# Entry of the up-projection: the copy of the third pair's product 5 ahead of the fifth pair's plain rounding on ACT

## The chip, the cores and the metric

The kernel runs on one core of one Trainium2 chip. The metric is the device time of one execution in microseconds; the median of three runs of the kernel before is 912.32 us.

## What the kernel computes

One layer of a streaming encoder on 512 tokens of width 1024: a recurrent branch and an attention branch, merged and projected, then a feed-forward block. The part that matters here is the beginning of the feed-forward block:

```
h = rms_norm(x, ffn_norm_pre[layer])
up = jnp.einsum("bsd,df->bsf", h, w_up[layer])          # 1024 -> 6144 columns
up = causal_dwconv(up, conv_f_w[layer], conv_f_b[layer]) # 3 taps over the tokens
gate, val = jnp.split(up, 2, axis=-1)
ffn_out = jnp.einsum("bsf,fd->bsd", jax.nn.gelu(gate) * val, w_down[layer])
x = x + rms_norm(ffn_out, ffn_norm_post[layer])
```

Of the kernel before, what the change touches and what calls it, by code (L numbers as in the profile page):

```python
# [63 lines left out]
def kernel(  # L64
# [263 lines left out]
    X, Y = slice(0, SH), slice(SH, S)  # L328
# [593 lines left out]
    with ExitStack() as g2:  # L922
# [17 lines left out]
        p, n = gp[0], gp[1]  # L940
# [239 lines left out]
    with ExitStack() as mix:  # L1180
# [116 lines left out]
        with ExitStack() as later:  # L1297
            for i in turned[NT - 1]:
                later.enter_context(tc.issue_after(i.ins))
            p = pairs[NU]  # L1300
# [61 lines left out]
    def first_tap(j):  # L1362
        fe[j] = [tap(e, first[2 * j + i][0], t) for i, (e, t) in enumerate(((j, "cg"), (j + JF, "cv")))]

    def first_taps(j, *which):
        for i in which or (0, 1):
            taps(j + JF * i, first[2 * j + i][0], fe[j][i])
# [7 lines left out]
    p, n = pairs[NU], pairs[NU + 1]  # L1375
# [18 lines left out]
    p.add(p.a[:, X], p.a[:, X], 2)  # L1394
    first_tap(0)
    n.sums_lo(1)
    m.plain_low(0)
    m.plain_high(0)
    p.p5()
    p.keep(1, p.c[:, X])  # L1400
    first_taps(2)
    first_taps(0, 0)
    m.sums(0)
# [64 lines left out]
    with man2:  # L1468
# [3 lines left out]
        b, p = pairs.pop(JF - 2), pairs.pop(JF - 1)  # L1472
# [274 lines left out]
```

## The kernel before

Every float32 operand of a product is split into a high half (rounded) and a low half (the rest), and each product is three matmuls: high by high, high by low, low by high. The result lies with channels on the 128 partitions and tokens along the free axis.

The 48 column blocks of the up-projection, each 128 wide, are worked on as 24 pairs: block j of the gate with block j + 24 of the value. Pairs 0 to 2 are computed plainly (their banks are `up0`, `up24`, `up1`, `up25`, `up2`, `up26`). From pair 3 on, a pair is computed by a two-by-two scheme with seven products in place of eight, over the halves of the contraction and of the tokens (X is the first 256 tokens, Y the last 256). Each of the seven products is 12 matmuls of 128x128 by 128x256: eight that use a high weight half (lines 429 and 430, alternating) and four that use a low one (line 432). Pairs 3, 4 and 5 are called p, n and m at the entry of this stage. In the names below the last number is the pair: `ml0_5` is a tile of pair 5; `th0_4` of pair 4. A number behind that, where there is one, only counts tiles.

Each pair has two PSUM banks, `a` (`up3` for pair 3) and `c` (`up27` for pair 3). What the code calls:

- `plain(i)`, that is `plain_low(i)` and `plain_high(i)`: the rounding of the untransformed weights. `plain_low(0)` makes ACT write the negated weights into `ml0` (line 364) and then makes GpSimd issue a DMA that adds the weights to it (line 365); `plain_high(0)` makes ACT write the rounded weights into `mh0` (line 380). Products 1 and 2 of a pair read `mh0` and `ml0`; product 3 reads `mh1` and `ml1`.
- `sums`, `sums_hi`, `sums_lo`: sums of weight blocks on DVE (`t`, line 325), their high halves on ACT (`th`, line 411) and low halves on DVE (`tl`, line 325). Products 4 to 7 read these.
- `p12`, `p5`, `product(n, ...)`: the matmuls. `p12` puts product 1 in `a[Y]` and product 2 in `a[X]`; `p5` puts product 5 in `c[X]`.
- `keep(i, ps)`: ACT copies a half bank into a tile `x` in SBUF (line 436), as that half bank is going to be accumulated further. `keep(2)` saves product 1, `keep(1)` saves product 5, `keep(0)` saves the sum after product 6.
- `add`: DVE adds a kept tile to a half bank (line 448).
- `tap`, `taps`: ACT starts the three-tap convolution out of PSUM (line 1325), DVE adds the other two taps (line 1331). `first_tap`, `first_taps` and `first_glu` do this for pairs 0 to 2.

From here on the order is written out by hand: instructions go to their engines in the order in which the code issues them. At the entry it is (lines 1396 to 1402, after `p.p12()`, `p.keep(2, ...)`, the add, `first_tap(0)` and `n.sums_lo(1)`):

```
    m.plain_low(0)
    m.plain_high(0)
    p.p5()
    p.keep(1, p.c[:, X])
    first_taps(2)
    first_taps(0, 0)
    m.sums(0)
```

Then a loop runs `period` (line 454) once for each pair. For pair 3 it issues product 6 into `a[Y]`, `keep(0)`, `n1.plain(1)` (nothing is left to do of it here, pair 4's is done), product 3 into `c[X]`, pair 4's `p12` and `keep(2)`, and product 7. For each later pair it issues `p5`, the adds of the pair before, the tap of the bank before, `keep(1)`, product 6, `keep(0)`, product 4 of the pair before, product 3, the next pair's `p12` and product 7. Product 3 accumulates onto product 5 in `c[X]`, so it has to wait until `keep(1)` has read that half bank.

## Time and profile before

| | |
|---|---|
| median of 3 runs | 912.32 us (912.11 to 912.33) |
| the profiled execution's own time | 910.93 us |
| its span (first to last instruction) | 909.2 us |
| PE (matmul) busy | 899.7 us, 99% of the span |
| DVE busy | 736.5 us, 81% |
| ACT busy | 596.3 us, 66% |
| POOL (GpSimd) busy | 214.8 us, 24% |
| granted TensorE clock | 0.999 of full speed |

The span leaves out 1.73 us of the profiled execution's time, and the profiled execution is 1.39 us shorter than the median of the runs. Times in the rows of the profile are microseconds from the span's start. PE is TensorE's matmul side, PEld its weight loads. In a row of the timeline stand the start, the duration, the engine, the line, the operation, what is written and read, how many instructions were merged, and in brackets the idle time of the engine before it with what ended it. The ends of matmuls are modelled.

### The profile page before, as it was taken

Reading aid. Unit: us, or ns where it says so; the run is one execution under the profiler, and the core shown is the slowest. Engines: PE = TensorE matmul, PEld = TensorE weight load, DVE = VectorE, ACT = ScalarE, POOL = GpSimd, SP = SyncE. Lnnn points to the kernel's source line nnn. Section 1 sums busy time; section 2 is a strip of 40 time slices with the busy share of each in tenths; the row PEclk is TensorE's granted clock in tenths of the full one; section 3 lists DMA queues with packets and bytes.
Section 4 is the critical chain, followed back from the end, with each engine's and each line's share of the span. In section 5 each row is a group of like instructions: output and inputs, shape, how many; then the busy total and the mean of one; then the engine's idle time right before and its main releaser. Section 6 shows DMA issues by size and latency. Waiting matters only on the chain.

```text
span 909.2 us, 15828 instructions
## 1 busy us (share of the span) xinstructions
PE 899.7 (99%) x5858; PEld 801.4 (88%) x5858; DVE 736.5 (81%) x1204; ACT 596.3 (66%) x1032; POOL 214.8 (24%) x276
## 2 busy tenths in 40 slices
PE   9999999999999999999999999999999999999997
PEld 8888888878899998888888889999999999988886
DVE  6975469538878749888868588989999999889897
ACT  7564595333466648776654487878888888677564
POOL 3244335544110112212104100233323223100000
PEclk9999999999999999999999999999999999999999
DMA  6777589989865378444515664678888988699764
GB/s 261 263 237 195 159 221 272 247 215 197 196 161 161 101 245 280 143 143 149 177 45 183 200 185 139 140 185 209 235 210 215 244 203 210 209 400 324 244 203 145
DMA packets 71040, 185.24 MB, mean 204 GB/s; under 512 B 7153, under 2 KB 27681, under 8 KB 70578
## 3 DMA queue, kind: packets, MB, share of 16 engines
q1 hardware_dynamic: 47360, 127.72, 42.0%
q0 software_dynamic: 23456, 56.37, 28.7%
q8 instruction: 46, 0.75, 0.3%
q14 instruction: 32, 0.26, 0.1%
q10 hardware_dynamic: 146, 0.14, 0.0%
HBM read 150.69 MB, written 35.73 MB: 205 GB/s over the span
## 4 chain that ended last, share of the span: by engine, by line
PE 98%; ACT 1%; DMA 1%; DVE 0%; issue 0%; SPq 0%; DVEq 0%
PE up L429 7%; PE up L430 7%; PE up L432 7%; PE dn L1455 4%; PE dn L1456 4%; PE dn L1454 4%; PE ga L220 2%; PE ga L219 2%; PE pa L220 2%; PE pa L218 2%; PE pa L219 2%; PE ga L218 2%; PE k L218 2%; PE q L218 2%; PE wo L1170 2%; PE pb L218 2%
## 5 line engine op out<-in xcount | busy, mean ns | idle before, releaser
L1331 DVE SCALAR_TENSOR_TENSOR u<-up,cpt,u 128x511 f32<-128x511 f32 x96 | 71.3, 745 | 3.5 <-ACT u L1325 1.8
L365 POOL DMA_DIRECT2D ml<-raw_up x42 | 36.2, 863 | 153.6 <-ACT ml L364 87.2
L1456 PE MATMUL dn<-wh_dn,al 128*128 128x512 f32 (+1 forms) x180 | 67.6, 376 | 0.0
L1455 PE MATMUL dn<-wl_dn,ah 128*128 128x512 f32 (+1 forms) x180 | 67.5, 375 | 0.0
L1454 PE MATMUL dn<-wh_dn,ah 128*128 128x512 f32 (+1 forms) x180 | 67.5, 375 | 0.0
L429 PE MATMUL up<-sh,th 128*128 128x256 f32 x252 | 60.2, 276 | 0.0
L430 PE MATMUL up<-sl,th 128*128 128x256 f32 x252 | 60.2, 276 | 0.0
L175 DVE TENSOR_TENSOR wl_dn<-raw_dn,wh_dn 128x1024 fp32r<-128x1024 f32 x42 | 51.1, 1217 | 8.2 <-ACT wh_dn L172 8.2
L172 ACT CAST wh_dn<-raw_dn 128x1024 fp32r<-128x1024 f32 x42 | 44.1, 1051 | 20.2 <-issue 8.0
L1325 ACT ACTIVATE u<-up,cpt 128x512 f32<-128x512 f32 x48 | 37.0, 779 | 21.7 <-PE up L432 11.9
L325 DVE TENSOR_TENSOR tl<-t,th 128x1024 fp32r<-128x1024 f32 x42 | 51.1, 1217 | 0.0
L429 PEld LDWEIGHTS up<-sh,th 128*128 128x128 f32 x252 | 47.3, 188 | 0.0
L430 PEld LDWEIGHTS up<-sl,th 128*128 128x128 f32 x252 | 47.3, 188 | 0.0
L1339 POOL TENSOR_TENSOR yf<-u,u 128x512 f32<-128x512 f32 x23 | 30.7, 1334 | 62.8 <-issue 48.2
L411 ACT CAST th<-t 128x1024 fp32r<-128x1024 f32 x42 | 43.7, 1044 | 2.5 <-DVE t L325 0.4
L429 PE MATMUL up<-h2h,mh 128*128 128x256 f32 x168 | 40.2, 276 | 0.0
L430 PE MATMUL up<-h2l,mh 128*128 128x256 f32 x168 | 40.2, 276 | 0.0
L1456 PEld LDWEIGHTS dn<-wh_dn,al 128*128 128x128 f32 x180 | 33.9, 188 | 6.3 <-DVE al L325 0.3
L1454 PEld LDWEIGHTS dn<-wh_dn,ah 128*128 128x128 f32 x180 | 33.9, 188 | 6.1
L1455 PEld LDWEIGHTS dn<-wl_dn,ah 128*128 128x128 f32 x180 | 33.9, 188 | 6.0
L432 PE MATMUL up<-sh,tl 128*128 128x256 f32 x252 | 38.8, 276 | 0.0
L1015 ACT ACTIVATE P<-P,mx 128x384 f32<-128x384 f32 (+3 forms) x64 | 35.2, 553 | 5.1 <-DVE mx L1010 4.2
(724 smaller groups left out, 3218.9 us busy)
## 6 DMA issues: line engine op xcount, KB each, us to landing
raw_up<-in_w_up_dram SPq DMA_DIRECT2D x48, 512.0 KB, 5.4
td<-in_w_down_dram POOLq DMA_DIRECT2D x36, 512.0 KB, 6.3
raw_dn<-td SPq DMA_DIRECT2D x24, 512.0 KB, 5.3
ml<-raw_up POOLq DMA_DIRECT2D x21, 512.0 KB, 5.5
B<-cnd POOLq DMA_DIRECT2D x16, 640.0 KB, 5.4
raw_dn<-in_w_down_dram SPq DMA_DIRECT2D x18, 512.0 KB, 4.2
raw_wo<-in_w_out_dram SPq DMA_DIRECT2D x16, 512.0 KB, 4.3
td<-td POOLq DMA_DIRECT2D x12, 512.0 KB, 11.2
```

What stands on the lines that cost most here:

```text
L172: act.copy(self.wh, self.raw)
L175: engine.tensor_tensor(out=self.wl, in0=self.raw, in1=self.wh.bitcast(F32), op=ALU.subtract)
L218: pe.matmul(dst, ah, bh, start=first, stop=False)
L325: dve.tensor_tensor(out=out, in0=a, in1=b, op=ALU.subtract)
L411: act.copy(self.th[i], self.t[i])
L429: pe.matmul(dst, wh[:, k], ah[:, k], start=first and k == 0, stop=False, skip_group_check=True)
L430: pe.matmul(dst, wh[:, k], al[:, k], start=False, stop=False, skip_group_check=True)
L432: pe.matmul(dst, wl[:, k], ah[:, k], start=False, stop=k == KH - 1, skip_group_check=True)
L1331: dve.scalar_tensor_tensor(out=c[:, s:], in0=ps[:, : S - s], scalar=col(C_CFW + 3 * e + j), in1=c[:, s:], op0=ALU.mult, op1=ALU.add)
L1454: pe.matmul(d[:, x], ah[:, k, tok], wh[:, k, x], start=first, stop=False, skip_group_check=True)
L1455: pe.matmul(d[:, x], ah[:, k, tok], wl[:, k, x], start=False, stop=False, skip_group_check=True)
L1456: pe.matmul(d[:, x], al[:, k, tok], wh[:, k, x], start=False, stop=last, skip_group_check=True)
```

## The change

Two lines are moved. The matmuls of pair 3's product 5 and the copy `keep(1)` are issued ahead of pair 5's plain rounding, where they stood behind it.

```
     first_tap(0)
     n.sums_lo(1)
+    p.p5()
+    p.keep(1, p.c[:, X])
     m.plain_low(0)
     m.plain_high(0)
-    p.p5()
-    p.keep(1, p.c[:, X])
     first_taps(2)
     first_taps(0, 0)
```

On ACT, at the entry of the up-projection (`u0` and `u24` are pair 0's taps, `up27` is bank `c` of pair 3, `x1_3` the copy of its product 5, `x0_3` the copy of bank `a` after product 6, `x2_4` the copy of pair 4's product 1):

```order
 L1325 ACTIVATE u0_6819<-up0_6243,cpt_79 128x512
 L1325 ACTIVATE u24_6821<-up24_6268,cpt_79 128x512
-L364 ACTIVATE ml0_5_6825<-raw_up5_6777 128x1024
-L380 CAST mh0_5_6828<-raw_up5_6777 128x1024
-L436 COPY x1_3_6843<-up27_6830 128x256
+L436 COPY x1_3_6838<-up27_6825 128x256
+L364 ACTIVATE ml0_5_6840<-raw_up5_6777 128x1024
+L380 CAST mh0_5_6843<-raw_up5_6777 128x1024
 L436 COPY x0_3_6866<-up3_6791 128x256
 L436 COPY x2_4_6905<-up4_6880 128x256
```

The copy of product 5 moved ahead of two instructions, and these two moved behind one; all else on ACT stands as before.

On POOL, at the same place (`ml0_5` is the DMA that completes the low half whose rounding moved on ACT; `yf` are the products of gate and value of pairs 1, 2 and 0):

```order
 L365 DMA ml1_4_6772<-raw_up28_6527 128x512
 L1339 TENSOR_TENSOR yf1_6788<-u1_6756,u25_6758 128x512
-L365 DMA ml0_5_6825<-raw_up5_6777 128x1024
+L365 DMA ml0_5_6840<-raw_up5_6777 128x1024
 L1339 TENSOR_TENSOR yf2_6911<-u2_6764,u26_6766 128x512
 L1339 TENSOR_TENSOR yf0_6915<-u0_6819,u24_6821 128x512
```

Nothing moved there but the numbers that count tiles, since the DMA stands between the same two instructions. PE, DVE and SP (the queue of plain loads) also keep their order.

More of the change, by code (lines that the diff above doesn't have):

```diff
@@ L1396 @@
     n.sums_lo(1)
+    p.p5()
+    p.keep(1, p.c[:, X])
     m.plain_low(0)
     m.plain_high(0)
-    p.p5()
-    p.keep(1, p.c[:, X])
     first_taps(2)
```

## Prediction

> **What bounds the kernel now.** I read the chain that ended last first, then the waits of PE from the up-projection on, then the busy time of each engine by stretches.
>
> The chain, by engine:
>
> ```profile
> PE 98%; ACT 1%; DMA 1%; DVE 0%; issue 0%; SPq 0%; DVEq 0%
> ```
>
> The kernel ends when TensorE has gone through its matmuls, so a microsecond counts only if PE stands still for it. ACT's 1% is small, and the question is whether this change touches a piece of it. The list of PE's waits from 540 us to the end (engine, line, what it waited for, total, times, longest) has one row:
>
> ```profile
> PE up L429 <- ACT x L436: 1.2, 1, 1.2
> ```
>
> It is a matmul of line 429 that waited for a copy of line 436, once. The busy times of the stretches show what surrounds it (start and end, length, then busy time per engine with the number of instructions):
>
> ```profile
> 565.00:592.00 27.00, 25.76 (x228) 25.56 (x226) 24.83 (x37) 23.68 (x35) 5.66 (x6) 1.00 0.60 142
> 592.00:660.00 68.00, 68.00 (x597) 68.00 (x598) 62.15 (x94) 53.34 (x84) 21.25 (x21) 1.00 0.83 212
> 660.00:725.00 65.00, 65.00 (x574) 65.00 (x572) 60.40 (x90) 54.07 (x82) 20.75 (x21) 1.00 0.87 219
> 725.00:790.00 65.00, 65.00 (x561) 64.52 (x560) 59.11 (x85) 50.68 (x78) 18.34 (x17) 1.00 0.79 207
> 790.00:860.00 70.00, 70.00 (x311) 57.78 (x311) 61.48 (x77) 49.10 (x68) 0.61 (x2) 1.00 0.92 320
> ```
>
> PE is short of full by 27.00 - 25.76 = 1.24 us before 592 and by nothing from 592 to 860. So there is one hole in this half of the kernel, and behind it a stage that runs at PE's own pace. The timeline of PE shows the hole (start, duration):
>
> ```profile
> 588.75 0.62 PE L432 MATMUL up<-sh,tl 128*128 128x256 f32 x4
> 589.20 0.28 PE L429 MATMUL up<-sh,th 128*128 128x256 f32 x1
> 590.11 0.62 PE L432 MATMUL up<-sh,tl 128*128 128x256 f32 x4
> 591.97 0.38 PE L429 MATMUL up<-sh,mh 128*128 128x256 f32 x1 [1.24 <-ACT x L436]
> 592.19 0.28 PE L430 MATMUL up<-sl,mh 128*128 128x256 f32 x1
> 593.47 0.28 PE L429 MATMUL up<-h2h,mh 128*128 128x256 f32 x1
> ```
>
> The first row is the end of pair 3's product 5, the second starts product 6 and the third ends it, the fourth starts product 3, and the last starts pair 4's product 1. The same stretch on ACT:
>
> ```profile
> 588.04 0.37 ACT L436 COPY x<-up 128x256 f32<-128x256 f32 x1 [1.38 <-PE up L432]
> 588.31 1.46 ACT L1325 ACTIVATE u<-up,cpt 128x512 f32<-128x512 f32 x2
> 589.65 1.06 ACT L364 ACTIVATE ml<-raw_up 128x1024 fp32r<-128x1024 f32 x1
> 590.60 1.04 ACT L380 CAST mh<-raw_up 128x1024 fp32r<-128x1024 f32 x1
> 591.53 0.66 ACT L436 COPY x<-up 128x256 f32<-128x256 f32 x2
> 596.38 0.37 ACT L436 COPY x<-up 128x256 f32<-128x256 f32 x1 [4.20 <-PE up L432]
> ```
>
> Product 5's last matmul ends, as modelled, at 588.75 + 0.62 = 589.37, but its copy starts only at 591.53, behind the two instructions of pair 5's rounding. Product 3 starts 0.44 us after that copy's start. A copy is 0.37 us long, so it is the first of the two copies that releases PE, not the second: the pair of them ends at 591.53 + 0.66 = 592.19, when PE is already running.
>
> **The change part by part.** *The hole.* The four line-432 matmuls that end product 5 start at 588.75 and product 6 starts at 589.20, so such a group takes 0.45 us. Product 3 could therefore start at 590.11 + 0.45 = 590.56. It starts at 591.97, so the hole in start times is 591.97 - 590.56 = 1.41 us (the 1.24 us of the wait are less because the modelled end of the last matmul overlaps). The first matmul after the hole also hands over late. The next pair's product 3 runs without a hole and gives the normal step:
>
> ```profile
> 601.63 0.28 PE L429 MATMUL up<-sh,mh 128*128 128x256 f32 x1
> 601.75 0.28 PE L430 MATMUL up<-sl,mh 128*128 128x256 f32 x1
> ```
>
> There the second matmul starts 0.12 us after the first, behind the hole 592.19 - 591.97 = 0.22 us after it, so the hole costs another 0.10 us. Together 1.51 us.
>
> *Where the copy lands.* It takes the slot of the rounding, 589.65 us. Its source is there: product 5 ended at 589.37, 0.28 us earlier. It ends at 589.65 + 0.37 = 590.02. PE started 591.97 - (591.53 + 0.37) = 0.07 us after the copy's end, so product 3 may start from 590.09, and its turn comes at 590.56. The margin is 0.47 us, and the hole goes entirely. The ready time of product 5 rests on a modelled matmul end. How good the model is shows at the copy before, `keep(2)`, and the matmuls that it waited for:
>
> ```profile
> 587.39 0.62 PE L432 MATMUL up<-h2h,ml 128*128 128x256 f32 x4
> ```
>
> They end at 587.39 + 0.62 = 588.01 and the copy starts at 588.04, so the model is good to 0.03 us here. The Trainium skill, page "Perfetto Trace Analysis", section "Tensor Engine Instruction (MATMUL, LD_WEIGHTS)", warns that the profiler estimates a matmul's end from its size and does not observe it. By that page the 0.28 us could be less than they look; by the row they hold, and an error of up to 0.47 us in the copy's start would cost nothing.
>
> *The rounding, moved back by one copy.* The rows that this part uses are the start of product 5, the DMA of `ml0_5`, all DMAs of line 365 with their least, median and longest time from issue to landing, and the first use of `ml0_5`:
>
> ```profile
> 587.84 0.28 PE L429 MATMUL up<-sh,th 128*128 128x256 f32 x1
> 591.01 0.88 POOL L365 DMA_DIRECT2D ml<-raw_up  x1 [2.97 <-PE up L432]
> L365 POOL DMA_DIRECT2D ml<-raw_up x42: 849/861/904, 570.2 to 770.8; - x42
> DMA to landing us min/median/max: 3.2/5.9/8.7
> 603.93 0.62 PE L432 MATMUL up<-h2h,ml 128*128 128x256 f32 x4
> ```
>
> Two instructions in a row on ACT start closer than their durations: the copy at 588.04 was followed at 588.31, 0.27 us later. So `ml0_5` starts at 589.65 + 0.27 = 589.92, `mh0_5` at 590.60 + 0.27 = 590.87, and the copy `keep(0)` behind them at about 591.80, where the second of the pair of copies ran before. Product 7, which overwrites what `keep(0)` reads, comes after pair 4's `p12`, which itself starts at 593.47 - 1.51 = 591.96 and takes two products of 1.36 us (product 5 starts at 587.84 and product 6 at 589.20). `keep(0)` ends by 592.2 and is covered by 2.5 us.
>
> The rounding brings its DMA with it. POOL issued it at 591.01, 0.30 us after `ml0_5` ended on ACT (589.65 + 1.06 = 590.71); the PE release named in the row was past by then too. Now it is issued at 591.28. What is queued behind it on POOL are the products `yf2` and `yf0`, which wait for gelus that stand on ACT behind the copy of 596.38. The first reader of `ml0_5` are the line-432 matmuls of pair 5's product 1, at 603.93 before and at 602.42 now. That leaves 602.42 - 591.28 = 11.1 us against a longest landing of 8.7 us (over these 42 transfers and 8 of the same line in an earlier stage). Cost: nothing. SP is not passed by anything.
>
> *What is late next.* PE comes 1.51 us earlier, and everything that feeds it has to follow. DVE is the engine with the least room:
>
> ```profile
> 594.84 0.69 DVE L325 TENSOR_TENSOR t<-raw_up 128x512 f32<-128x512 f32 x1
> 596.79 0.43 DVE L448 TENSOR_TENSOR up<-up,x 128x256 f32<-128x256 f32 x1 [1.26 <-ACT x L436]
> 598.57 0.89 DVE L448 TENSOR_TENSOR up<-up,x 128x256 f32<-128x256 f32 x2
> 616.87 0.90 DVE L448 TENSOR_TENSOR up<-up,x 128x256 f32<-128x256 f32 x2 [0.52 <-PE up L432]
> ```
>
> DVE was free at 594.84 + 0.69 = 595.53 and then waited 1.26 us for pair 4's `keep(2)`. It can come forward by those 1.26 us and no more, so it is then 0.25 us later in relation to PE. That could show in two places: product 4 of pair 3 (the first row), which overwrites what the first add at 598.57 reads, and product 3 of pair 4, which waits for the copy (the second row) behind a tap on ACT that waits for those adds:
>
> ```profile
> 600.27 0.28 PE L429 MATMUL up<-h2h,th 128*128 128x256 f32 x1
> 600.24 0.36 ACT L436 COPY x<-up 128x256 f32<-128x256 f32 x1
> ```
>
> The first add ends at about 598.57 + 0.43 = 599.00 and product 4 starts at 600.27, 1.27 us later; now 1.02 us. The copy ends at 600.60 and product 3 starts at 601.63, 1.03 us later; now 0.78 us. Both covers hold. In each later period DVE has 0.52 us to spare (the row at 616.87), so the 0.25 us are made up within one. Cost: nothing.
>
> *Sum.* -1.41 - 0.10 = -1.51 us on the profiled execution, 910.93 to 909.42 us. PE's order behind the hole is unchanged and it has no other wait, so I let all of it reach the end. On the median that is 912.32 - 1.51 = 910.81 us, 0.17% less. About 0.2%, or 1.82 us, is what a measurement of this kernel can tell from no change, so the expected gain is just inside that bound.
>
> **The rivals.** *Nothing is gained: product 3 needs the second copy too.* Then it is released at 592.2 as before, and the time stays 912.3 us. For it: both copies stand together at 591.53. Against it: PE ran at 591.97, before the second ended. 3%.
>
> *Part of the gain is given back* by DVE or ACT being late in the first periods. Its price lies between nothing and about 1.26 us, which is what DVE's idle time before the add took up and no longer can; in the middle, 0.6 us, the time is 911.4 us. It decides once a lag exceeds 0.78 us, and I count 0.25 us. 8%.
>
> *Slower: the low half of pair 5 lands late.* The DMA of `ml0_5` is now issued later while its reader comes earlier. It decides from a landing time of 11.1 us. For it: DMAs that POOL issued in an earlier stage, for sums of the down-projection's weights, took longer at their worst. Their row:
>
> ```profile
> DMA to landing us min/median/max: 3.9/6.3/14.9
> ```
>
> With 14.9 us it would land at 606.18, PE would wait 606.18 - 602.42 = 3.76 us, and the kernel would lose 3.76 - 1.51 = 2.25 us: 914.6 us. Against it: none of the `ml` transfers took over 8.7 us. 7%.
>
> *More than the hole.* The timed runs are 912.32 - 910.93 = 1.39 us longer than the profiled execution, and the profile can't say where. If that sits in this wait, as it would if the copy were released later there, the gain is 1.51 + 1.39 = 2.90 us: 909.4 us. A lower clock after the hole would be another way, but the stretch from 592 on has a granted clock of 1.00 and the matmul at 592.19 is back at 0.28 us. 17%.
>
> **How the numbers follow.** The forecast has the rest, 65%: 910.8 us. The range of 910.2 to 911.9 us takes in the forecast with 0.6 us on the fast side (the beginning of the last rival) and up to 1.1 us given back; outside are most of the last rival, the unchanged case and the slow one, some 2 in 10. Faster by over 0.2% is the last rival, 0.17. Within 0.2% are the forecast, the given-back and the unchanged case, 0.65 + 0.08 + 0.03 = 0.76. Slower is the late DMA, 0.07.
>
> **What would show it.** In the changed profile ACT's copy stands at about 589.7 with no idle time before it and the rounding at 589.9; the waits of PE from 540 us on have no row for line 436; product 3 starts at about 590.6 and pair 4's product 1 at about 592.0; the add of pair 4 waits less than 0.3 us on DVE; the span is about 907.7 us. The forecast is wrong if PE gets a wait at products 3 or 4 of the next periods or at the low half of pair 5, if the copy at 589.7 waits for PE, or if the 1.5 us are there at 600 us and gone at the end.

## The result, and the profile after

The changed kernel takes 909.98 us in the median of 20 runs (909.32 to 911.78); the kernel before, run again beside it, takes 911.97 us in 20 runs (910.86 to 913.49). The ratio is 0.998, with a 95% interval of 0.9974 to 0.9987: 1.99 us less, between 1.2 and 2.4 us. The forecast was 1.51 us less, but of a median of 912.32 us, and 909.98 us lies below its range of 910.2 to 911.9 us.

The profiled execution of the changed kernel is the longest of its 20 (911.78 us), so it has to be read in parts. The waits of PE, all over the kernel, from the changed kernel (engine, line, what it waited for, total, times, longest):

```profile
PE tr_p L246 <- DVE xn L619: 2.1, 2, 1.2
PE xa L596 <- POOL ident masks.py:199: 1.5, 1, 1.5
```

The wait for the copy of line 436 is gone, and no other has come up in the up-projection or behind it. The two that are left are in the first 10 us of the kernel; the upper one is not in the profile of before. PE's timeline of the changed kernel at the entry:

```profile
590.24 0.28 PE L429 MATMUL up<-sh,th 128*128 128x256 f32 x1
592.51 0.62 PE L432 MATMUL up<-sh,tl 128*128 128x256 f32 x4
592.96 0.28 PE L429 MATMUL up<-sh,mh 128*128 128x256 f32 x1
593.08 0.28 PE L430 MATMUL up<-sl,mh 128*128 128x256 f32 x1
```

Product 5 starts at 590.24, that is 2.40 us later than the 587.84 of before; this comes from the first 15 us (below). Product 3 follows product 6 at 592.96, 0.45 us behind the start of its last group and without a hole; less 2.40 us that is 590.56, the turn that the prediction gave it. The second matmul starts 0.12 us behind the first. ACT's timeline of the changed kernel:

```profile
590.71 1.46 ACT L1325 ACTIVATE u<-up,cpt 128x512 f32<-128x512 f32 x2
592.05 0.38 ACT L436 COPY x<-up 128x256 f32<-128x256 f32 x1
592.30 1.09 ACT L364 ACTIVATE ml<-raw_up 128x1024 fp32r<-128x1024 f32 x1
593.26 1.06 ACT L380 CAST mh<-raw_up 128x1024 fp32r<-128x1024 f32 x1
594.20 0.39 ACT L436 COPY x<-up 128x256 f32<-128x256 f32 x1
```

The copy starts at 592.05 without idle time before it, the rounding at 592.30 and 593.26 and `keep(0)` at 594.20. Less 2.40 us: 589.65, 589.90, 590.86 and 591.80, against 589.65, 589.92, 590.87 and 591.80 in the prediction. The first line below is POOL's DMA of `ml0_5`, the second DVE's add of pair 4:

```profile
593.68 0.88 POOL L365 DMA_DIRECT2D ml<-raw_up  x1 [3.25 <-ACT ml L364]
597.85 0.43 DVE L448 TENSOR_TENSOR up<-up,x 128x256 f32<-128x256 f32 x1
```

593.68 - 2.40 = 591.28 us is the predicted issue. DVE no longer waits for its add at all, where it waited 1.26 us before.

What the change is worth from the entry on can be read off within one execution, from product 5's start to the start of the last matmul. The last matmul of before and of the changed kernel:

```profile
902.27 0.28 PE L1456 MATMUL dn<-wh_dn,al 128*128 128x256 f32 x1
```

```profile
903.13 0.28 PE L1456 MATMUL dn<-wh_dn,al 128*128 128x256 f32 x1
```

902.27 - 587.84 = 314.43 us before, 903.13 - 590.24 = 312.89 us after: 1.54 us less. I use this stretch for every kernel below. It ends at the start of the last matmul; the 321.3 and 319.8 us that two expectations name run on to the end of the span (909.2 - 587.84 = 321.4 us before), so only differences can be compared with them.

### The profile page after: what moved, and what is told of

Same layout as the page of the kernel before. It is cut to its first block, busy times and chain, and to the rows that moved or that the text cites. A ratio compares the mean times of both kernels' runs of the same rounds, so it can differ in the third digit from the quotient of the medians.

```text
span 910.0 us, 15828 instructions
## 1 busy us (share of the span) xinstructions
PE 899.8 (99%) x5858; PEld 801.7 (88%) x5858; DVE 736.5 (81%) x1204; ACT 596.4 (66%) x1032; POOL 214.4 (24%) x276
## 4 chain that ended last, share of the span: by engine, by line
PE 98%; DMA 1%; DVE 0%; ACT 0%; issue 0%; DVEq 0%; SPq 0%
PE up L430 7%; PE up L432 7%; PE up L429 7%; PE dn L1455 4%; PE dn L1456 4%; PE dn L1454 4%; PE ga L220 2%; PE ga L219 2%; PE pa L220 2%; PE pa L218 2%; PE pa L219 2%; PE ga L218 2%; PE k L218 2%; PE q L218 2%; PE wo L1170 2%; PE k L219 2%
```

## The experiments

Theory A is that only the hole counts, 1.51 us, and that the rest of the 1.99 us is scatter between runs. Theory B is that the timed runs gain more by the change than one trace shows, the last rival of the prediction. All kernels were timed against the kernel before, which had a median of 911.52 us beside the first four (27 runs) and of 911.74 us beside the other four (31 runs). The ratio given with each run is not the quotient of these medians, so the two can differ a little.

**A part of the change: the copy between the two roundings.**

```
     m.plain_low(0)
-    m.plain_high(0)
     p.p5()
     p.keep(1, p.c[:, X])
+    m.plain_high(0)
```

> The copy of product 5 stands between the two roundings of pair 5: behind ml0_5, ahead of mh0_5. Theory A (the hole is all that counts): on the clock of the trace of before the copy starts at 590.60, ends at 590.97 and releases product 3 at 591.04, 0.48 us after its turn at 590.56; with 0.10 us for restarting the hole is 0.58 us where before has 1.51, so from product 5's start to the end the trace is 0.93 us shorter than before and the median about 0.9 us less. Theory B (the timed runs gain a third more than the trace shows, as 1.99 us against 1.51 would say): the median is 1.2 us less. Theory C (product 3 needs the copy of product 6's sum too): no gain.

Measured: 910.90 us (11 runs), ratio 0.9993 (0.9984 to 1.0002). From its trace, PE's timeline with product 5, product 3 and the last matmul:

```profile
589.57 0.28 PE L429 MATMUL up<-sh,th 128*128 128x256 f32 x1
592.76 0.39 PE L429 MATMUL up<-sh,mh 128*128 128x256 f32 x1 [0.30 <-ACT x L436]
903.04 0.28 PE L1456 MATMUL dn<-wh_dn,al 128*128 128x256 f32 x1
```

A wait of 0.30 us is left, and the stretch is 313.47 us, 0.96 us less than before (0.93 expected) where the whole change gives 1.54. Theory C, that product 3 needs the second copy too, falls. The medians differ by 0.6 us, with an interval from 1.5 us less to 0.2 us more, which holds both A's 0.9 and B's 1.2.

**The other way: the hole widened.** The rounding of `mh0_5` is done a second time ahead of the copy.

```
     m.plain_high(0)
+    act.copy(m.w[1][0].rearrange("p k e -> p (k e)"), m.r[0][:, A])
+    act.copy(m.w[2][0].rearrange("p k e -> p (k e)"), m.r[0][:, B])
     p.p5()
```

> The order of before, with the rounding of mh0_5 done a second time in two halves on ACT ahead of the copy (the same values are written again). Each half is 0.61 us long and hands over after about 0.52 us, so the copy starts 1.04 us later. Theory A: the hole of 1.51 us becomes 2.55 us, PE's wait in the list 2.3 us, the time from product 5's start to the end grows by 1.04 us and so does the median. Theory B: the median grows by 1.4 us. If instead the work behind the hole could catch up, less than 1.0 us.

Measured: 915.00 us (5 runs, 914.36 to 915.62), ratio 1.0036 (1.0024 to 1.0049). That is 3.5 us more, not 1.0 or 1.4. The trace, first PE's timeline, then the busy time by stretches with the granted clock behind POOL's column:

```profile
594.29 0.39 PE L429 MATMUL up<-sh,mh 128*128 128x256 f32 x1 [2.41 <-ACT x L436]
595.35 1.03 PE L432 MATMUL up<-sh,ml 128*128 128x256 f32 x4
596.18 0.41 PE L429 MATMUL up<-h2h,mh 128*128 128x256 f32 x1
```

```profile
590.00:595.00 5.00, 2.59 (x23) 2.39 (x22) 4.89 (x8) 4.48 (x8) 0.88 (x1) 1.00 0.54 167
595.00:600.00 5.00, 5.00 (x32) 5.00 (x31) 1.69 (x3) 0.00 (x0) 0.00 (x0) 0.66 0.60 129
600.00:605.00 5.00, 5.00 (x46) 5.00 (x45) 3.27 (x6) 3.94 (x8) 3.38 (x3) 1.00 0.14 54
```

The hole is 2.41 us by the wait. In the five microseconds behind it the mean clock is 0.66, which is 0.34 x 5 = 1.7 us of matmul time, and a matmul takes 0.41 us in place of 0.28. Asked for in shorter stretches, the trace shows half the clock for 3.4 us and then all of it:

```profile
595.36:598.78 3.42, 3.42 (x19) 3.42 (x18) 1.32 (x3) 0.00 (x0) 0.00 (x0) 0.50 0.71 143
598.78:602.19 3.41, 3.41 (x32) 3.41 (x32) 1.41 (x3) 1.84 (x4) 0.86 (x1) 1.00 0.02 5
```

The stretch from product 5 to the last matmul tells the same:

```profile
589.00 0.28 PE L429 MATMUL up<-sh,th 128*128 128x256 f32 x1
906.34 0.28 PE L1458 MATMUL dn<-wh_dn,al 128*128 128x256 f32 x1
```

It is 317.34 us, 2.91 us more than before: 1.2 us for the wait (2.41 against 1.24) and 1.7 us for the clock. The expectation lacked the clock. The other 0.6 us of the 3.5 us between the medians lie outside the stretch or in the scatter of five runs; the interval of the ratio, 2.2 to 4.5 us, holds 2.9.

**Half as much more**, to see whether the hole of before is itself near that edge.

```
     m.plain_high(0)
+    act.copy(m.w[1][0].rearrange("p k e -> p (k e)"), m.r[0][:, A])
     p.p5()
```

> The order of before with one half of mh0_5 rounded a second time ahead of the copy (the same values are written again): the hole grows by 0.52 us to 1.93 us, between that of before (1.41 us, clock 1.00 behind it) and the widened one (2.58 us, a clock of 0.66 in the five microseconds from 595). If the clock stays up: 0.5 us more than before. If the gate closes: that and 1.7 us or more, 2.2 us over before, or both kinds of executions.

Measured: 913.61 us (9 runs, 912.18 to 916.53), ratio 1.002 (1.001 to 1.003). Its trace, first PE's wait, then the stretches with the granted clock, then product 5 and the last matmul:

```profile
PE up L429 <- ACT x L436: 1.9, 1, 1.9
```

```profile
590.00:595.00 5.00, 4.09 (x37) 3.89 (x35) 3.16 (x5) 3.63 (x6) 1.91 (x2) 1.00 0.58 144
595.00:600.00 5.00, 4.02 (x22) 4.03 (x23) 3.82 (x6) 1.17 (x4) 0.24 (x1) 0.69 1.00 241
```

```profile
591.20 0.28 PE L429 MATMUL up<-sh,th 128*128 128x256 f32 x1
907.85 0.28 PE L1457 MATMUL dn<-wh_dn,al 128*128 128x256 f32 x1
```

The clock falls behind this hole too, and the stretch is 316.65 us, 2.2 us more than before. Here as well it is half the clock for 3.4 us:

```profile
596.85:600.27 3.42, 3.42 (x18) 3.42 (x18) 2.00 (x4) 0.00 (x0) 0.00 (x0) 0.50 1.07 271
```

The traced execution is the longest of the nine. For the other eight there are only their times, and these look like both kinds of executions: two took 912.18 and 912.22 us, which is the 0.5 us of the wider hole over 911.74, the others 913.19 to 914.89 us. Their mean clocks (0.999 and 0.998 for the two, 0.994 to 0.997 for the others) do not settle it. Half the clock for 3.4 us is less than 0.002 of such a mean, and the runs of the kernel before beside them range from 0.995 to 0.999. The Trainium skill, page "TensorE: Matmul & The Clock Gate", section "What's actually happening", has the gate close after an idle window of about 3.4 us and the windows run free of the kernel. The 3.4 us at half the clock agree with a window of that length, and two kinds of executions, if that is what the times show, would agree with free-running windows; the idle time does not agree, since 1.9 us of waiting closed the gate here. In both traces of the order of before (the second is shown further down) a wait of 1.2 us did not.

**Both roundings in their usual place of the loop**, behind both copies.

```
-    m.plain_low(0)
-    m.plain_high(0)
     p.p5()
     p.keep(1, p.c[:, X])
```

> The two roundings of pair 5 are taken out of the entry; the loop issues them in its usual place, so on ACT they stand behind both copies, and the DMA of ml0_5 is issued 1.1 us later than in the changed kernel. Theory A: no hole, the same as the changed kernel, 1.5 us less than before; the DMA has 10 us where 6 are usual. Late-DMA rival: a wait of PE at the low matmuls of pair 5's product 1, and less gain by its length.

Measured: 910.41 us (11 runs), ratio 0.9985 (0.9976 to 0.9994). Its trace shows the DMA of `ml0_5` on POOL and then product 5 and the last matmul on PE:

```profile
593.36 0.87 POOL L365 DMA_DIRECT2D ml<-raw_up  x1 [4.36 <-PE up L432]
```

```profile
588.80 0.28 PE L429 MATMUL up<-sh,th 128*128 128x256 f32 x1
901.75 0.28 PE L1454 MATMUL dn<-wh_dn,al 128*128 128x256 f32 x1
```

PE has no wait from the entry on, and the stretch is 312.95 us, 1.48 us less than before. The DMA is issued 593.36 - 588.80 = 4.56 us behind product 5's start, 1.1 us later than in the changed kernel (593.68 - 590.24 = 3.44), and PE does not notice. The late-DMA rival has no footing.

**The copy at the head**, even before pair 0's taps, where it has to wait for PE.

```
+    p.p5()
+    p.keep(1, p.c[:, X])
     first_tap(0)
     n.sums_lo(1)
     m.plain_low(0)
     m.plain_high(0)
-    p.p5()
-    p.keep(1, p.c[:, X])
```

> The copy of product 5 stands even ahead of the two taps of pair 0 on ACT (and product 5's matmuls are issued ahead of them). ACT then waits for PE at the copy: free at 588.41 on the clock of before, product 5 ends at 589.37, so a wait of about 1.0 us on ACT, and taps and roundings 1.3 us later than in the changed kernel less the 0.3 us of the copy. Theory A: PE does not wait, 1.5 us less than before, since what ACT does late has over 1 us of cover. Rival: the taps come late for DVE and through it for product 4 of pair 3, and part of the 1.5 us is given back.

Measured: 910.10 us (11 runs), ratio 0.9987 (0.9978 to 0.9996). In its trace, ACT's copy, the end of product 5 that it waited for, then product 5's start and the last matmul:

```profile
589.52 0.37 ACT L436 COPY x<-up 128x256 f32<-128x256 f32 x1 [0.99 <-PE up L432]
```

```profile
588.87 0.62 PE L432 MATMUL up<-sh,tl 128*128 128x256 f32 x4
```

```profile
587.96 0.28 PE L429 MATMUL up<-sh,th 128*128 128x256 f32 x1
900.94 0.28 PE L1456 MATMUL dn<-wh_dn,al 128*128 128x256 f32 x1
```

ACT stands still for 0.99 us, as expected, and it costs nothing: 312.98 us, 1.45 us less than before. As the copy waits for product 5 here, it also tests the modelled end on which the prediction's 0.28 us rested: 588.87 + 0.62 = 589.49 us, and the copy starts 0.03 us later. Every place tried for the copy ahead of both roundings gives the whole gain.

**The two kernels again.** The kernel before against itself, and the changed kernel a second time, neither with an edit.

> The kernel before, unchanged, timed against itself. If the difference of 1.99 us between the medians is 1.5 us of the hole and the rest the scatter of runs, the two medians here may be some 0.3 to 0.5 us apart with nothing changed, and in its trace the hole is 1.41 us again, the time from product 5's start to the end 321.3 us, while the time at which product 5 starts differs from the 587.84 us of before. If the hole closed PE's clock gate in part of the executions, some executions of it would have a lower clock behind the hole, as the widened hole's trace has.

> The changed kernel a second time. Theory A (the hole is all that counts): a median 1.5 us below that of before, nearer to it than 1.99 us; from product 5's start to the end 319.8 us. Theory B (the timed runs gain more than the trace shows): again 2.0 us or more.

The kernel before against itself: 911.60 us (11 runs) beside 911.74, ratio 1.0003 (0.9994 to 1.0012). The changed kernel: 910.17 us (11 runs), ratio 0.9985 (0.9976 to 0.9993), 1.57 us less and not 1.99. Product 5 and the last matmul on PE's timeline, first of the kernel before in this second trace (with product 3 between them), then of the changed one:

```profile
588.70 0.28 PE L429 MATMUL up<-sh,th 128*128 128x256 f32 x1
592.83 0.38 PE L429 MATMUL up<-sh,mh 128*128 128x256 f32 x1 [1.25 <-ACT x L436]
903.44 0.28 PE L1456 MATMUL dn<-wh_dn,al 128*128 128x256 f32 x1
```

```profile
588.32 0.28 PE L429 MATMUL up<-sh,th 128*128 128x256 f32 x1
901.34 0.28 PE L1456 MATMUL dn<-wh_dn,al 128*128 128x256 f32 x1
```

The stretches are 314.74 and 313.02 us long. Behind the hole the second trace of the kernel before has a full clock:

```profile
595.00:600.00 5.00, 5.00 (x47) 5.00 (x46) 3.67 (x8) 2.45 (x5) 1.56 (x2) 1.00 0.23 44
```

The stretch repeats within 0.3 us in these traces. It is 314.43 and 314.74 us with the hole, and 312.89, 313.02, 312.95 and 312.98 us in the four traces without it: 1.4 to 1.9 us apart, the means 314.59 and 312.96, 1.63 us. The start of product 5 repeats much worse: 587.84 and 588.70 us with the same kernel, 590.24 and 588.32 us with the changed one.

**More warming at the start**, on the changed kernel.

```
-                spin(1)
+                spin(3)
                 sumsq_whole(0)
...
+                spin(3)
                 for g in range(2):
                     scaled(1, g)
                     turn(1, g)
```

> The changed kernel with more of the matmuls that only keep PE busy at the very start: three instead of one behind the gain's matmuls, and three more between the two first groups of transposes. If the scatter between executions comes from the clock in the first 15 us, the spread of the runs narrows or the median moves; the time from product 5's start to the end stays 319.8 us. As the added matmuls can also hold up the transposes by up to 1.5 us, the median may go either way by 1 us.

Measured: 911.69 us (11 runs, 909.45 to 913.34), ratio 1.0001 (0.9992 to 1.0009). Product 5 and the last matmul in its trace:

```profile
587.47 0.28 PE L429 MATMUL up<-sh,th 128*128 128x256 f32 x1
900.79 0.28 PE L1457 MATMUL dn<-wh_dn,al 128*128 128x256 f32 x1
```

The stretch is 313.32 us, that of the changed kernel within 0.4 us, and this execution, the fastest of the eleven, reached product 5 earlier than any other traced. But the spread of the runs widened to 3.9 us and the gain is gone in the median. A change in the first 15 us alone has thus moved the median by 1.5 us (911.69 against 910.17). None of the slower runs was traced, and that the start is what scatters the other kernels' runs is not shown by it.

## Why the prediction was wrong

The mechanism was right at every point that can be read: the copy's slot and its readiness, the hole closed in full, the 0.10 us of restarting, the rounding 0.25 us later (0.27 predicted), the DMA at 591.28 on the clock of before, DVE without a wait, and no new wait of PE from the entry on. The sum of -1.51 us measured -1.54 us in the two profiled executions and -1.6 us over six traces. That it came within 0.03 us is partly luck, as the stretch itself repeats only within 0.3 us. The rivals of no gain, of a gain given back and of the late DMA are excluded, by the copy placed between the roundings, by the stretch that stays the same when ACT is held up, and by the DMA issued another 1.1 us later.

What failed is the size of one term and the range, not the mechanism: the step "On the median that is 912.32 - 1.51 = 910.81 us", which starts from a median that was too high, and the range built on it. The forecast is 0.83 us above the 909.98 measured. Of these, 912.32 - 911.97 = 0.35 us are the starting value: a median of three runs that lay within 0.22 us of each other, where 20 runs spread over 2.6 us. The other 1.99 - 1.51 = 0.48 us are the difference of two medians, whose interval of 1.2 to 2.4 us holds 1.51; the second measurement gave 1.57. The fast side of the range, 0.6 us, was half the width of that interval, and left no room for a starting value that was itself 0.35 us off. The 1.99 us also lie just beyond the 1.82 us that the prediction took as the bound of a clear gain, to which it gave a chance of 0.17 by its last rival, a longer hole in the timed runs. No trace shows that: in the second trace of the kernel before, an execution of 912.09 us, the wait was 1.25 us again.

Theory B isn't needed: taking all 31 runs of the changed kernel against the 89 of the one before (20, 27 and 31 beside the others, 11 against itself), the medians are 909.99 and 911.72 us, 1.73 us apart, between the 1.54 us of the traces and the first 1.99. A few tenths beyond 1.54 us can't be excluded. The prediction took the 1.39 us between profiled and timed runs for something that may sit in the wait; they are within the spread of single runs instead. At least part of that spread arises at the start. In the changed kernel's first trace, the busy times of a stretch in the first 15 us, two groups of eight matmuls and the first matmul of line 230, which follows the start:

```profile
8.10:14.90 6.80, 5.63 (x27) 5.21 (x26) 4.61 (x9) 6.16 (x11) 4.21 (x2) 0.50 1.01 393
11.26 2.08 PE L638 MATMUL xa<-hh,wh_xa 128*128 128x256 f32 x8
13.13 1.91 PE L638 MATMUL xa<-hl,wh_xa 128*128 128x256 f32 x8
15.86 0.28 PE L230 MATMUL xa<-hh,wh_xa 128*128 128x256 f32 x1
```

The same of its second trace:

```profile
8.10:14.90 6.80, 6.80 (x44) 6.58 (x43) 4.82 (x9) 5.92 (x12) 4.83 (x2) 1.00 1.01 395
10.52 1.94 PE L638 MATMUL xa<-hh,wh_xa 128*128 128x256 f32 x8
12.29 1.10 PE L638 MATMUL xa<-hl,wh_xa 128*128 128x256 f32 x8
14.18 0.28 PE L230 MATMUL xa<-hh,wh_xa 128*128 128x256 f32 x1
```

With the same instructions, PE got through 27 matmuls in the first trace and 44 in the second. In the first the clock was at half throughout, and in its first 10 us PE also waited 2.1 us for DVE (the first row of the waits in the section on the result). The 1.00 of the second can't be right for its whole stretch: the first eight matmuls take 1.94 us there, nearly as long as the same eight at half the clock, and only the next eight are fast, with 1.10 us in place of 1.91. So within this stretch PE was slow at first in both traces; it became fast at about 12.3 us in the second, and only at the end of the stretch in the first. Line 230 was reached 15.86 - 14.18 = 1.68 us later in the first, and product 5 590.24 - 588.32 = 1.92 us later.

## What to carry to other kernels

When PE waits once, look in the queue of the engine that it waits for: work that nobody needs soon stood ahead of a copy that released PE, and swapping them returned the whole hole. Price such a change between two marks inside one trace, but before putting a range around a total, find out how far single runs of the kernel lie apart; three that agree don't tell.

A hole in PE's work can cost more than its length. Here 1.24 us of waiting left the clock up in both traces, and 1.9 us brought it down in the one traced, for another 1.7 us by half the clock over 3.4 us. And where the clock column reads 1.00, see whether the matmuls are as short as elsewhere.

## What the runs showed that was not expected

The granted clock fell to half for 3.4 us behind holes of 1.9 and 2.4 us, in the middle of a stage in which PE was busy before and after. The price was 2.9 us in the stretch for a hole that had grown by only 1.2 us. Where between 1.24 and 1.9 us the edge lies, and whether it is the same in every execution, was not tried. It need not be a matter of the hole's length alone: at the start of the changed kernel's first trace the clock was 1.00 from 4.75 to 8.16 us and 0.50 from there to 14.99 us, with no single wait over 1.2 us, though there among other kinds of matmuls and transposes.
